# MoBA queries and keys with the rotary halves of four heads in two tiles, and some late steps of a decoder layer moved

## The chip, the cores and the metric

The kernel runs on one core of a Trainium2 chip. The metric is the device time of one execution in microseconds. The core has a matrix engine (TensorE, PE in the profile, with its weight loads shown as PEld), three engines for elementwise work (VectorE = DVE, ScalarE = ACT, GpSimd = POOL) and queues that start transfers (here those of SyncE = SP and of ACT). Each engine works through its own instructions in order and waits for the others by semaphores.

## What is computed

One layer over 512 tokens of width 1024, in float32. Two kinds of attention run side by side from the same normalised input, MoBA with rotary positions and stick-breaking without, with 8 heads of 64 each; they are gated, merged, and followed by a convolutional gated feed-forward of width 2816.

```python
h   = RMSNorm(x)
[q_a,k_a,v_a | q_b,k_b,v_b | gate_a,gate_b] = h @ W_in
y_a = MoBA(rope(q_a), rope(k_a), v_a)
y_b = stick_breaking(q_b, k_b, v_b)
m   = sigmoid(gate_a) * (y_a @ W_a) + sigmoid(gate_b) * (y_b @ W_b)
x   = x + m @ W_out
x   = x + ConvGLU(RMSNorm(x))
out = RMSNorm_final(x)

def rope(t, pos):                      # for each head, 64 wide
    t1, t2 = t[..., :32], t[..., 32:]
    return concat([t1*cos - t2*sin, t2*cos + t1*sin], axis=-1)
```

With 512 tokens and blocks of 256, MoBA's selection takes every past block, so it is causal softmax attention.

## The kernel before

**Number format.** Each float32 operand is split into a rounded part and a residue (`hi`, `lo`, in the format float32r), and each product is three matmuls, hi·hi, hi·lo and lo·hi (`mm3`, L71 to L74). Weights come from HBM in pieces of 128x1024 through `wload` (L55): a transfer to `raw`, a copy to `whi` on ScalarE (L67), the residue `wlo` on VectorE (L68). Three buffers each let the load run ahead of its use.

**Order.** TensorE runs in the order in which the program is written (`manual_schedule`). The order on the other engines is made by a scheduler that simulates the kernel; `tc.issue_after` ties instructions behind a given one on its engine.

**Stages.** (1) Loop over 8 tiles of the input (L161): each tile is scaled and split into `xg`, and 12 matmuls per tile (L184) build MoBA's q and k of the first two head pairs in four PSUM banks `qk0`. Squares of the input are summed in `ssq` (L159), from which `rstd_cols` (8 small matmuls, L117, then a square root and a Newton step) and `bcast_rows` (4 transposes, L136) make the norm `r1` and its broadcast `rb`. `NWARM` small matmuls (L150) run ahead of all this. (2) `vproj_a` projects MoBA's values. (3) Four calls of `attend` (L358), each for two pairs of heads: two of MoBA ("a"), two of stick-breaking ("b").

**One call of attend** goes through three units of query tiles. `score` makes the scores in PSUM tiles `sc`, then the weights with VectorE and ScalarE; `turn` transposes the weights of one pair on TensorE (L375) into a PSUM tile `tp`, of which there is one, and copies it out as `aT` on ScalarE (L378) or VectorE (L380). At the end come the products with the values (L393). After each step, `fill(gap)` issues other projections on TensorE: a filler unit is three 128x512 matmuls. The gaps stand in `GAPS_A`, `GAPS_A2` and `GAPS_B`, the fillers in a list (L424): MoBA's q and k of the other pairs, stick-breaking's q, k and values, and the first `NG` gates.

**MoBA's rotation** (`moba_half`, L256) works on one pair, its two heads one below the other in 128 partitions, the two halves of each head 32 partitions apart. The projection is copied from PSUM to `pc` (L258), four transfers on ScalarE's queue write it with the halves exchanged into `sw` (L261), and VectorE multiplies `pc` by cos (L263) and `sw` by signed sin (L264), adds them (L265) and `split_out` splits the sum (L249, L250). The scores of a head are then matmuls over 64 partitions, the two heads of a pair one after the other (L307).

**Afterwards**: the merge of the two branches (L454 on, with the remaining gates), the output projection, the second norm (`norm2`, L490, after the first up-projection), 44 up-projections with their convolution, and the down-projection. When the attention's PSUM pools close, new ones open: `pmm2` (6 banks) and `ptr2` (2 banks).

Of the kernel before, what the change touches and what calls it, by code (L numbers as in the profile page):

```python
# [10 lines left out]
F32 = mybir.dt.float32  # L11
# [12 lines left out]
FT = FF // 128  # L24
EPS = 1e-6
NG = 3
NWARM = 32
LAST = 4
WORDER = ([(n, k) for n in ("qk0", "va") for k in range(4)] + [("vb", g, h) for g in range(2) for h in range(2)]
          + [("mqk", p, n) for p in (2, 3) for n in range(2)] + [("sqk", p, n) for p in range(4) for n in range(2)]  # L30
          + [("g", i, b) for i in range(KT) for b in range(2)] + [("ab", i) for i in range(KT)]
          + [("out", i) for i in range(KT)] + [("up", i, b) for i in range(FT) for b in range(2)]
          + [("down", k) for k in range(FT)])
# [5 lines left out]
def trunk_layer(ctx: ExitStack, tc: tile.TileContext, xT: bass.AP, w: bass.AP, vec: bass.AP,  # L39
# [3 lines left out]
    def pool(stack, name, bufs, space=None, side=None):  # L43
        kw = {}
        if space is not None:
            kw["space"] = space
        if side is not None:
            kw["side"] = side
        return stack.enter_context(tc.tile_pool(name=name, bufs=bufs, reuse_waits="tile", **kw))
# [5 lines left out]
    def wload(key, pieces=1, dst=None, eng=None):  # L55
        raw = wraw.tile([128, 1024], F32, name="raw")
        hi = (dst or wsp).tile([128, 1024], F32R, name="whi")
        lo = (dst or wsp).tile([128, 1024], F32R, name="wlo")
        n = 1024 // pieces
        for i in range(pieces):  # L60
            sl = slice(i * n, (i + 1) * n)
            (eng if eng is not None and i == 0 else nc.sync).dma_start(raw[:, sl], w[WIDX[key]][:, sl])
            if eng is not None and i == 0:
                nc.scalar.preload_act_table_set("sqrt_and_others")
        for i in range(pieces):
            sl = slice(i * n, (i + 1) * n)
            nc.scalar.activation(hi[:, sl], raw[:, sl], AF.Copy)  # L67
            nc.vector.tensor_sub(lo[:, sl], raw[:, sl], hi[:, sl].bitcast(F32))  # L68
        return hi, lo
# [71 lines left out]

    st1 = ExitStack()
    xp = pool(st1, "xp", 6)
    swp0 = pool(st1, "swp0", 4)
    p1 = pool(st1, "p1", 1, PSUM)
    ssq = xp.tile([128, S], F32, name="ssq", bufs=1)
    qk0 = [p1.tile([128, S], F32, name=f"q{j}") for j in range(4)]
# [13 lines left out]
    for k in range(KT):  # L161
        xk = xks[k] = xp.tile([128, S + 1], F32, name="xk")
        nc.sync.dma_start(xk, xT[k])
        if k % 2 == 0:
            w0 = wload(("qk0", k // 2), 4 if k == 0 else 2, eng=nc.scalar if k == 0 else None)
        if k == 1:
            nc.sync.dma_start(vecs, vec)
        gm = xk[:, S:]
        if k == 0:
            nc.vector.tensor_scalar(xg[k][:, 0], xk[:, :S], gm, None, op0=OP.mult)  # L170
        else:
            xgi = nc.scalar.activation(xg[k][:, 0], xk[:, :S], AF.Copy, scale=gm)
        nc.vector.scalar_tensor_tensor(xg[k][:, 1], xk[:, :S], gm, xg[k][:, 0].bitcast(F32),
                                       op0=OP.mult, op1=OP.subtract)
        if k >= 3:
            with tc.issue_after(xgi.ins):
                square(k - 3)
        if k == KT - 1:
            for j in range(k - 2, KT):
                square(j)  # L180
            r1 = rstd_cols(ssq, pmm, "mm", "n1")
        for n, (i, j) in enumerate(((0, 0), (0, 1), (1, 0))):
            for c in range(4):
                nc.tensor.matmul(qk0[c], w0[i][:, (k % 2) * 512 + c * 128:(k % 2) * 512 + (c + 1) * 128],  # L184
                                 xg[k][:, j], start=(k == 0 and n == 0), stop=(k == KT - 1 and n == 2))
# [19 lines left out]
    mp = pool(mst, "mp", 1, side="right")  # L205
    va = mp.tile([128, QT, 512], F32, name="va")
    rt = pool(mst, "rt", 2, side="right")
    swp = pool(mst, "swp", 2, side="right")
    tg = mp.tile([128, 2, S], F32, name="tg")
    nc.sync.dma_start(tg, trig)  # L210
    for i in range(2):
# [36 lines left out]
    def split_out(hl, o):  # L248
        nc.scalar.activation(hl[:, 0], o, AF.Copy)  # L249
        nc.vector.tensor_sub(hl[:, 1], o, hl[:, 0].bitcast(F32))  # L250

    stk = {}

    mq = {}

    def moba_half(p, n, P, tmp):  # L256
        pc = tmp.tile([128, S], F32, name="pc")
        nc.scalar.activation(pc, P, AF.Copy, scale=(0.125, 1.0)[n])  # L258
        sw = tmp.tile([128, S], F32, name="sw")
        for r in range(0, 128, 32):  # L260
            nc.scalar.dma_start(sw[r:r + 32], pc[r ^ 32:(r ^ 32) + 32])  # L261
        m1 = rt.tile([128, S], F32, name="m1")
        nc.vector.tensor_mul(m1, pc, tg[:, 0])  # L263
        nc.vector.tensor_mul(sw, sw, tg[:, 1])  # L264
        nc.vector.tensor_add(m1, m1, sw)  # L265
        hl = mqkp.tile([128, 2, S], F32R, name=f"hl{n}")
        split_out(hl, m1)
        mq.setdefault(p, []).append(hl)
        if n:
            stk["a", p] = [(*mq[p], h * 64) for h in range(2)]  # L270

    def moba_qk(p):
        for n in range(2):
            yield from proj(("mqk", p, n), lambda ps: moba_half(p, n, ps, swp))

    def sb_qk(p):
        sc = {}
# [16 lines left out]
    def scores(br, pairs, seg):  # L294
        scs = [psc.tile([128, 2, 512], F32, name="sc") for _ in pairs]
        if br == "a":
            for sc in scs:
                for j, (qt, o, n) in enumerate(seg):
                    for h in range(2):
                        nc.tensor.matmul(sc[:, h, o + n - 128:o + n], identb, maskb, start=j == 0, stop=False,  # L300
                                         skip_group_check=True)
        for p, sc in zip(pairs, scs):
            for qt, o, n in seg:
                for m, (c, d) in enumerate(((0, 0), (0, 1), (1, 0))):
                    for h in range(2):
                        q, k, r0 = stk[br, p][h]
                        nc.tensor.matmul(sc[:, h, o:o + n], q[r0:r0 + 64, c, qt * 128:(qt + 1) * 128],  # L307
                                         k[r0:r0 + 64, d, :n], start=br == "b" and m == 0, stop=m == 2,
                                         skip_group_check=True)
        return scs  # L310

    def weights_a(sc, seg):
# [86 lines left out]
            nc.scalar.activation(y[:, 0], av[:, j], AF.Copy)  # L399
            nc.vector.tensor_sub(y[:, 1], av[:, j], y[:, 0].bitcast(F32))  # L400

    for p in range(2):
        for n in range(2):
            moba_half(p, n, qk0[2 * n + p], swp0)
    vproj_a()
    st1.close()
    atp = pool(asta, "atp", 2)
# [13 lines left out]
            yield from proj(("g", i, b), lambda ps: use(b, ps))  # L421

    pend = {}
    fillers = [moba_qk(2), moba_qk(3), sb_qk(0), sb_qk(1), vproj_b(0), sb_qk(2), sb_qk(3), vproj_b(1)]  # L424
    fillers += [gates(i) for i in range(NG)]
    GAPS_A = (14, 0, 4, 6, 0, 4, 8, 4, 4)
    GAPS_A2 = (10, 0, 3, 6, 0, 3, 6, 3, 3)
    GAPS_B = (8, 4, 4, 4, 4, 4, 8, 4, 4)
    attend("a", (0, 1), GAPS_A)
    attend("a", (2, 3), GAPS_A2)  # L430
    mst.close()
# [6 lines left out]
    fill(1000)  # L438
    psA.close()
    psB = ExitStack()  # L440
    pmm = pool(psB, "pmm2", 6, PSUM)
    ptr = pool(psB, "ptr2", 2, PSUM)
    asta.close()

    x1p = pool(ctx, "x1p", 1)
# [41 lines left out]
            nc.vector.tensor_add(ssq2, ssq2, sq)  # L487
    rb2 = x1s.tile([128, S], F32, name="rb2")

    def norm2():  # L490
        r2 = rstd_cols(ssq2, ptr, "tp", "n2")
        bcast_rows(r2, ptr, "tp", rb2)

    upq = [(i, b) for i in range(FT) for b in range(2)]

    def up_mm():
# [4 lines left out]
        return ps  # L501

    ups = [up_mm()]
    norm2()
    ups.append(up_mm())
    mst.close()
    gp = pool(ctx, "gp", 1)
    gT = [gp.tile([128, 2, S], F32R, name=f"gT{i}") for i in range(FT)]
# [73 lines left out]
def pack(w_in, w_a, w_b, w_out, w_up, w_down):  # L582
    def rows(m, c):
        return m[:, c].reshape(m.shape[0] // 128, 128, len(c)).transpose(1, 0, 2).reshape(128, -1)

    c128 = np.arange(128)
    t = {}
    first = np.concatenate([np.arange(256), 512 + np.arange(256)])
    for k in range(4):
        t["qk0", k] = rows(w_in[k * 256:(k + 1) * 256], first)  # L590
    for p in (2, 3):
        for n, base in enumerate((0, 512)):
            t["mqk", p, n] = rows(w_in, base + p * 128 + c128)
    for j in range(4):
        t["va", j] = rows(w_in[j * 256:(j + 1) * 256], 1024 + np.arange(512))
    for g in range(2):
        for h in range(2):
            t["vb", g, h] = rows(w_in[h * 512:(h + 1) * 512], 2560 + g * 256 + np.arange(256))
    for p in range(4):
        for n, base in enumerate((1536, 2048)):  # L600
            t["sqk", p, n] = rows(w_in, base + p * 128 + c128)
    for i in range(KT):
        for b in range(2):
            t["g", i, b] = rows(w_in, 3072 + b * 1024 + i * 128 + c128)
        t["ab", i] = np.concatenate([rows(w_a, i * 128 + c128), rows(w_b, i * 128 + c128)], axis=1)
        t["out", i] = rows(w_out, i * 128 + c128)
    for i in range(FT):
        for b in range(2):
            t["up", i, b] = rows(w_up, b * FF + i * 128 + c128)
        t["down", i] = w_down[i * 128:(i + 1) * 128]  # L610
    return np.ascontiguousarray(np.stack([t[k] for k in WORDER]))
# [29 lines left out]
```

## Time and profile before

| | us |
|---|---|
| median of 3 runs | 758.01 |
| lowest and highest of them | 757.87 and 759.09 |
| profiled execution | 759.67 |
| its span, first to last instruction | 757.6 |

The mean granted TensorE clock of the profiled execution is 0.995 of full. The profile lists, among other things, busy times, groups of instructions by line and form, waits between engines, busy times in chosen stretches (windows) and the timeline of one engine. A line such as `L264 DVE TENSOR_TENSOR sw<-sw,tg 128x512 ... x8 | 5.5, 691 | 8.3 <-DMA sw<-pc 8.3` reads: line 264, on VectorE, tile `sw` from `sw` and `tg`, 8 times; 5.5 us in all, 691 ns each on average; before them the engine was idle for 8.3 us, and what ended that was the transfer of `pc` to `sw`. All stretches are in microseconds from the start of the span.

### The profile page before, as it was taken

The numbers are of one execution on the slowest core, as the hardware profiler recorded it, in microseconds if no ns is written. First come the engines' busy times: TensorE is split into PE (matmuls) and PEld (weight loads), VectorE is DVE, ScalarE is ACT, GpSimd is POOL, SyncE is SP. The second block draws the span as 40 slices with busy tenths as digits, with TensorE's granted clock in tenths as the row PEclk, the third lists the DMA queues.
The fourth block names the chain that finished last, engine by engine and source line by source line (L and its number), as shares of the span: only waits on it lengthen the run. The fifth ranks groups of instructions, "written<-read, shape, count | busy, mean of one in ns | idle before, by whom it ended". The sixth has DMA issues, their size and how long they took to land.

```text
span 757.6 us, 9539 instructions
## 1 busy us (share of the span) xinstructions
PE 738.8 (98%) x3816; PEld 614.7 (81%) x3816; DVE 450.4 (59%) x638; ACT 310.0 (41%) x445; POOL 22.6 (3%) x40
## 2 busy tenths in 40 slices
PE   8999899999999999999989999999999999999996
PEld 7887788969887888888878888888888888888885
DVE  6676767494873544446557767677767773222233
ACT  6445445454662332324345444444444442121233
POOL 0000000220410000000000000000000000000000
PEclk9999999999999999999999999999999999999998
DMA  9433312021125223232322222323232323323203
GB/s 313 137 112 98 90 37 83 30 84 56 57 84 188 91 84 111 84 111 84 112 84 83 96 99 87 109 86 109 86 109 84 112 83 112 105 90 94 101 28 112
DMA packets 23900, 74.12 MB, mean 98 GB/s; under 512 B 2992, under 2 KB 3632, under 8 KB 23856
## 3 DMA queue, kind: packets, MB, share of 16 engines
q1 hardware_dynamic: 21600, 70.24, 27.7%
q10 hardware_dynamic: 2256, 3.28, 1.5%
q8 instruction: 30, 0.49, 0.3%
q14 instruction: 14, 0.11, 0.0%
HBM read 69.31 MB, written 2.10 MB: 94 GB/s over the span
## 4 chain that ended last, share of the span: by engine, by line
PE 73%; issue 20%; DVE 2%; ACT 2%; DMA 1%; POOL 1%; ACTq 0%; POOLq 0%; DVEq 0%
PE mm L72 18%; PE mm L73 18%; PE mm L74 18%; PE d L74 5%; PE d L72 5%; PE d L73 5%; PE q L184 3%; POOL a L338 1%; DMA sw<-pc 1%; DVE R L346 1%; PE tp L393 1%; ACT whi L67 1%; DMA raw<-w 0%; PE d L544 0%; PE tp L375 0%
## 5 line engine op out<-in xcount | busy, mean ns | idle before, releaser
L67 ACT ACTIVATE whi<-raw 128x1024 fp32r<-128x1024 f32 (+2 forms) x128 | 129.8, 1020 | 220.8 <-PE mm L73 78.9
L68 DVE TENSOR_TENSOR wlo<-raw,whi 128x1024 fp32r<-128x1024 f32 (+2 forms) x128 | 150.0, 1176 | 94.3 <-ACT whi L67 93.2
L72 PE MATMUL mm<-h,whi 128*128 128x512 f32 x352 | 137.0, 389 | 0.0
L74 PE MATMUL mm<-h,wlo 128*128 128x512 f32 x352 | 137.0, 389 | 0.0
L73 PE MATMUL mm<-h,whi 128*128 128x512 f32 x352 | 136.9, 389 | 0.0
L72 PE MATMUL mm<-xg,whi 128*128 128x512 f32 x224 | 90.4, 403 | 0.0
L73 PE MATMUL mm<-xg,whi 128*128 128x512 f32 x224 | 87.9, 392 | 0.0
L74 PE MATMUL mm<-xg,wlo 128*128 128x512 f32 x224 | 87.8, 392 | 0.0
L74 PEld LDWEIGHTS mm<-h,wlo 128*128 128x128 f32 x352 | 66.1, 188 | 13.8
L73 PEld LDWEIGHTS mm<-h,whi 128*128 128x128 f32 x352 | 66.1, 188 | 13.7
L72 PEld LDWEIGHTS mm<-h,whi 128*128 128x128 f32 x352 | 66.1, 188 | 13.5
L72 PE MATMUL d<-whi,gT 128*128 128x512 f32 x176 | 69.2, 393 | 0.0
L74 PE MATMUL d<-whi,gT 128*128 128x512 f32 x176 | 68.5, 389 | 0.0
L73 PE MATMUL d<-wlo,gT 128*128 128x512 f32 x176 | 68.5, 389 | 0.0
L517 DVE TENSOR_TENSOR u<-mm,rb 128x512 f32<-128x512 f32 x44 | 30.3, 689 | 41.2 <-PE mm L74 41.2
L72 PEld LDWEIGHTS mm<-xg,whi 128*128 128x128 f32 x224 | 42.5, 190 | 10.0 <-issue 1.4
L74 PEld LDWEIGHTS mm<-xg,wlo 128*128 128x128 f32 x224 | 42.3, 189 | 9.1
L73 PEld LDWEIGHTS mm<-xg,whi 128*128 128x128 f32 x224 | 42.4, 189 | 7.9
L249 ACT ACTIVATE gT<-t 128x512 fp32r<-128x512 f32 x22 | 13.9, 632 | 60.6 <-DVE t L526 60.6
L74 PEld LDWEIGHTS d<-whi,gT 128*128 128x128 f32 x176 | 33.0, 188 | 6.9
L73 PEld LDWEIGHTS d<-wlo,gT 128*128 128x128 f32 x176 | 33.1, 188 | 6.6
L72 PEld LDWEIGHTS d<-whi,gT 128*128 128x128 f32 x176 | 33.1, 188 | 6.4
(180 smaller groups left out, 1046.0 us busy)
## 6 DMA issues: line engine op xcount, KB each, us to landing
raw<-w SPq DMA_DIRECT2D x118, 512.0 KB, 3.3
xk<-xT SPq DMA_DIRECT2D x8, 256.5 KB, 5.4
sw<-pc ACTq DMA_DIRECT2D x32, 64.0 KB, 2.0
x1T<-xT SPq DMA_DIRECT2D x8, 256.0 KB, 5.0
raw<-w SPq DMA_DIRECT2D x6, 256.0 KB, 5.6
out<-on ACTq DMA_DIRECT2D x4, 256.0 KB, 2.7
out<-on SPq DMA_DIRECT2D x4, 256.0 KB, 2.5
tg<-trig SPq DMA_DIRECT2D x1, 512.0 KB, 6.2
```

The lines of the kernel that those rows point to most:

```text
L67: nc.scalar.activation(hi[:, sl], raw[:, sl], AF.Copy)
L68: nc.vector.tensor_sub(lo[:, sl], raw[:, sl], hi[:, sl].bitcast(F32))
L72: nc.tensor.matmul(ps, a[0], b[0], start=start, stop=False)
L73: nc.tensor.matmul(ps, a[0], b[1], start=False, stop=False)
L74: nc.tensor.matmul(ps, a[1], b[0], start=False, stop=stop)
L184: nc.tensor.matmul(qk0[c], w0[i][:, (k % 2) * 512 + c * 128:(k % 2) * 512 + (c + 1) * 128], xg[k][:, j], start=(k == 0 and n == 0), stop=( ...
L249: nc.scalar.activation(hl[:, 0], o, AF.Copy)
L338: nc.gpsimd.affine_select(out=zz, in_=zz, pattern=[[0, 2], [-1, 128]], compare_op=OP.is_ge, fill=fill, base=-1, channel_multiplier=1)
L346: nc.vector.tensor_tensor_scan(R[:, h, r0:r0 + n][:, ::-1], z[:, ::-1], z, 1.0, op0=OP.mult, op1=OP.bypass)
L393: nc.tensor.matmul(av[h * 64:(h + 1) * 64, j, qt * 128:(qt + 1) * 128], v[:, kb, (2 * p + h) * 64:(2 * p + h + 1) * 64], aT[p][:, h, o + k ...
L517: nc.vector.tensor_mul(u, ps, rb2)
```

## The change

- The weights of MoBA's q and k are packed so that one projection holds the first halves of four heads (32 partitions each) and another the second halves. `rotate` multiplies each by cos and by sin straight from PSUM, and when both are there, forms the difference and the sum and splits them. Copy, exchange transfers and `swp` pools are gone.
- MoBA's scores (in `scores`) are matmuls over 32 partitions, four heads in turn, three products for each of the two halves, into four PSUM banks.
- The first weight load is issued after the first tile's split; `NWARM` goes from 32 to 36; `rstd_cols` of the first norm moves behind four matmuls of the last tile; the transposes of the second norm move behind the second up-projection; `ptr2` is opened ahead of `pmm2`; some gaps differ.

```diff
-NWARM = 32
+NWARM = 36
...
     for k in range(KT):
...
-        if k % 2 == 0:
-            w0 = wload(("qk0", k // 2), 4 if k == 0 else 2, eng=nc.scalar if k == 0 else None)
...
         if k == 0:
             nc.vector.tensor_scalar(xg[k][:, 0], xk[:, :S], gm, None, op0=OP.mult)
         else:
+            if k % 2 == 0:
+                w0 = wload(("qk0", k // 2), 2)
             xgi = nc.scalar.activation(xg[k][:, 0], xk[:, :S], AF.Copy, scale=gm)
-        nc.vector.scalar_tensor_tensor(...)
+        xlo = nc.vector.scalar_tensor_tensor(...)
+        if k == 0:
+            with tc.issue_after(xlo.ins):
+                w0 = wload(("qk0", 0), 4, eng=nc.scalar)
...
-            r1 = rstd_cols(ssq, pmm, "mm", "n1")
         for n, (i, j) in enumerate(((0, 0), (0, 1), (1, 0))):
+            if k == KT - 1 and n == 1:
+                r1 = rstd_cols(ssq, pmm, "mm", "n1")
...
-    def moba_half(p, n, P, tmp):
-        pc = tmp.tile([128, S], F32, name="pc")
-        nc.scalar.activation(pc, P, AF.Copy, scale=(0.125, 1.0)[n])
-        sw = tmp.tile([128, S], F32, name="sw")
-        for r in range(0, 128, 32):
-            nc.scalar.dma_start(sw[r:r + 32], pc[r ^ 32:(r ^ 32) + 32])
-        m1 = rt.tile([128, S], F32, name="m1")
-        nc.vector.tensor_mul(m1, pc, tg[:, 0])
-        nc.vector.tensor_mul(sw, sw, tg[:, 1])
-        nc.vector.tensor_add(m1, m1, sw)
-        hl = mqkp.tile([128, 2, S], F32R, name=f"hl{n}")
-        split_out(hl, m1)
...
+    def rotate(g, n, i, ps, half):
+        sc = (0.125, 1.0)[n]
+        half[i] = [rt.tile([128, S], F32, name=f"r{i}{j}") for j in range(2)]
+        for j in range(2):
+            nc.vector.scalar_tensor_tensor(half[i][j], ps, sc, tg[:, j], op0=OP.mult, op1=OP.mult)
+        if i:
+            out = []
+            for j, op in ((0, nc.vector.tensor_sub), (1, nc.vector.tensor_add)):
+                o = half[0][j]
+                op(o, o, half[1][1 - j])
+                hl = mqkp.tile([128, 2, S], F32R, name=f"hl{j}")
+                split_out(hl, o)
+                out.append(hl)
+            stk.setdefault(("a", g), []).append(out)
+
+    def moba_qk(g):
+        for n in range(2):
+            half = {}
+            for i in range(2):
+                yield from proj(("mqk", n, i), lambda ps: rotate(g, n, i, ps, half))
...
+            Q, K = stk["a", pairs[0] // 2]
+            for qt, o, n in seg:
+                for i in range(2):
+                    for m, (c, d) in enumerate(((0, 0), (0, 1), (1, 0))):
+                        for h in range(4):
+                            r0 = h * 32
+                            nc.tensor.matmul(scs[h // 2][:, h % 2, o:o + n],
+                                             Q[i][r0:r0 + 32, c, qt * 128:(qt + 1) * 128], K[i][r0:r0 + 32, d, :n],
+                                             start=False, stop=i == 1 and m == 2, skip_group_check=True,
+                                             tile_position=(r0, 0))
+            return scs
...
-    fillers = [moba_qk(2), moba_qk(3), sb_qk(0), sb_qk(1), vproj_b(0), sb_qk(2), sb_qk(3), vproj_b(1)]
+    fillers = [moba_qk(1), sb_qk(0), sb_qk(1), vproj_b(0), sb_qk(2), sb_qk(3), vproj_b(1)]
...
-    GAPS_A = (14, 0, 4, 6, 0, 4, 8, 4, 4)
+    GAPS_A = (12, 0, 5, 5, 0, 5, 7, 5, 5)
     GAPS_A2 = (10, 0, 3, 6, 0, 3, 6, 3, 3)
-    GAPS_B = (8, 4, 4, 4, 4, 4, 8, 4, 4)
+    GAPS_B = (8, 4, 5, 4, 3, 5, 7, 5, 5)
...
+    ptr = pool(psB, "ptr2", 2, PSUM)
     pmm = pool(psB, "pmm2", 6, PSUM)
-    ptr = pool(psB, "ptr2", 2, PSUM)
...
     ups = [up_mm()]
-    norm2()
+    r2 = rstd_cols(ssq2, ptr, "tp", "n2")
     ups.append(up_mm())
+    bcast_rows(r2, ptr, "tp", rb2)
...
-    first = np.concatenate([np.arange(256), 512 + np.arange(256)])
+    def halves(base, g, i):
+        return base + (4 * g + c128 // 32) * 64 + 32 * i + c128 % 32
+
+    first = np.concatenate([halves(base, 0, i) for base in (0, 512) for i in range(2)])
```

More of the change, by code (lines that the diff above doesn't have):

```diff
@@ L26 @@
 NG = 3
-NWARM = 32
+NWARM = 36
 LAST = 4
 WORDER = ([(n, k) for n in ("qk0", "va") for k in range(4)] + [("vb", g, h) for g in range(2) for h in range(2)]
-          + [("mqk", p, n) for p in (2, 3) for n in range(2)] + [("sqk", p, n) for p in range(4) for n in range(2)]
+          + [("mqk", n, i) for n in range(2) for i in range(2)] + [("sqk", p, n) for p in range(4) for n in range(2)]
           + [("g", i, b) for i in range(KT) for b in range(2)] + [("ab", i) for i in range(KT)]
@@ L143, in trunk_layer @@
     xp = pool(st1, "xp", 6)
-    swp0 = pool(st1, "swp0", 4)
     p1 = pool(st1, "p1", 1, PSUM)
@@ L171, in trunk_layer @@
         else:
+            if k % 2 == 0:
+                w0 = wload(("qk0", k // 2), 2)
             xgi = nc.scalar.activation(xg[k][:, 0], xk[:, :S], AF.Copy, scale=gm)
-        nc.vector.scalar_tensor_tensor(xg[k][:, 1], xk[:, :S], gm, xg[k][:, 0].bitcast(F32),
-                                       op0=OP.mult, op1=OP.subtract)
+        xlo = nc.vector.scalar_tensor_tensor(xg[k][:, 1], xk[:, :S], gm, xg[k][:, 0].bitcast(F32),
+                                             op0=OP.mult, op1=OP.subtract)
+        if k == 0:
+            with tc.issue_after(xlo.ins):
+                w0 = wload(("qk0", 0), 4, eng=nc.scalar)
         if k >= 3:
@@ L207, in trunk_layer @@
     rt = pool(mst, "rt", 2, side="right")
-    swp = pool(mst, "swp", 2, side="right")
     tg = mp.tile([128, 2, S], F32, name="tg")
@@ L252, in trunk_layer @@
     stk = {}
-    mq = {}
-    def moba_half(p, n, P, tmp):
-        pc = tmp.tile([128, S], F32, name="pc")
-        nc.scalar.activation(pc, P, AF.Copy, scale=(0.125, 1.0)[n])
-        sw = tmp.tile([128, S], F32, name="sw")
-        for r in range(0, 128, 32):
-            nc.scalar.dma_start(sw[r:r + 32], pc[r ^ 32:(r ^ 32) + 32])
-        m1 = rt.tile([128, S], F32, name="m1")
-        nc.vector.tensor_mul(m1, pc, tg[:, 0])
-        nc.vector.tensor_mul(sw, sw, tg[:, 1])
-        nc.vector.tensor_add(m1, m1, sw)
-        hl = mqkp.tile([128, 2, S], F32R, name=f"hl{n}")
-        split_out(hl, m1)
[L268 to L272, printed above, removed]
+    def rotate(g, n, i, ps, half):
[13 more added lines that the diff above has]
+    def moba_qk(g):
         for n in range(2):
-            yield from proj(("mqk", p, n), lambda ps: moba_half(p, n, ps, swp))
+            half = {}
+            for i in range(2):
+                yield from proj(("mqk", n, i), lambda ps: rotate(g, n, i, ps, half))
     def sb_qk(p):
@@ L307, in scores @@
                         nc.tensor.matmul(sc[:, h, o:o + n], q[r0:r0 + 64, c, qt * 128:(qt + 1) * 128],
-                                         k[r0:r0 + 64, d, :n], start=br == "b" and m == 0, stop=m == 2,
-                                         skip_group_check=True)
+                                         k[r0:r0 + 64, d, :n], start=m == 0, stop=m == 2, skip_group_check=True)
         return scs
@@ L400, in attend @@
             nc.vector.tensor_sub(y[:, 1], av[:, j], y[:, 0].bitcast(F32))
-    for p in range(2):
-        for n in range(2):
-            moba_half(p, n, qk0[2 * n + p], swp0)
+    for n in range(2):
+        half = {}
+        for i in range(2):
+            rotate(0, n, i, qk0[2 * n + i], half)
     vproj_a()
@@ L488, in trunk_layer @@
     rb2 = x1s.tile([128, S], F32, name="rb2")
-    def norm2():
-        r2 = rstd_cols(ssq2, ptr, "tp", "n2")
-        bcast_rows(r2, ptr, "tp", rb2)
     upq = [(i, b) for i in range(FT) for b in range(2)]
@@ L587, in pack @@
     t = {}
-    first = np.concatenate([np.arange(256), 512 + np.arange(256)])
+    def halves(base, g, i):
+        return base + (4 * g + c128 // 32) * 64 + 32 * i + c128 % 32
+    first = np.concatenate([halves(base, 0, i) for base in (0, 512) for i in range(2)])
     for k in range(4):
         t["qk0", k] = rows(w_in[k * 256:(k + 1) * 256], first)
-    for p in (2, 3):
-        for n, base in enumerate((0, 512)):
-            t["mqk", p, n] = rows(w_in, base + p * 128 + c128)
+    for n, base in enumerate((0, 512)):
+        for i in range(2):
+            t["mqk", n, i] = rows(w_in, halves(base, 1, i))
     for j in range(4):
@@ L629 @@
     ang = np.tile(inv, 4)[:, None] * np.arange(S, dtype=np.float32)[None, :]
-    sign = np.where(np.arange(128) % 64 < 32, -1, 1).astype(np.float32)[:, None]
-    trig = np.ascontiguousarray(np.stack([np.cos(ang), sign * np.sin(ang)], axis=1).astype(np.float32))
+    trig = np.ascontiguousarray(np.stack([np.cos(ang), np.sin(ang)], axis=1).astype(np.float32))
     arrays = {"xT": xT, "w": w, "vec": vec, "gfin": np.ascontiguousarray(a["g_final"]), "trig": trig}
```

## The prediction

> **What bounds the kernel now.** I read the page's busy times first.
>
> ```profile
> PE 738.8 (98%) x3816; PEld 614.7 (81%) x3816; DVE 450.4 (59%) x638; ACT 310.0 (41%) x445; POOL 22.6 (3%) x40
> ```
>
> TensorE (PE) is busy for 98% of the span. Matmuls follow one another without a pause nearly everywhere, so an engine other than PE matters only where it makes PE wait. The price of a plain matmul and one of those waits stand in the chain of work that ended last (start, duration, what).
>
> ```profile
> 387.97 0.23 PE mm L73
> 388.20 0.23 PE mm L74
> ...
> 390.67 1.28 ACT L124
> 391.96 0.21 ACT n2s L124
> ...
> 393.03 0.65 PE tp L136 x4
> ```
>
> One 128x512 matmul advances the chain by 0.23 us, so a projection of 24 takes 5.5 us and one unit of filler (three matmuls) 0.68 us. The second view is the waits of PE alone (total, times, longest).
>
> ```profile
> PE tp L375 <- ACT aT L378: 3.9, 3, 2.0
> PE tp L136 <- DVE n2r L130: 2.5, 1, 2.5
> PE tp L375 <- DVE aT L380: 1.9, 1, 1.9
> PE q L184 <- ACT whi L67: 1.1, 1, 1.1
> PE mm L72 <- DVE g L416: 0.8, 1, 0.8
> PE tp L393 <- DVE aT L380: 0.6, 1, 0.6
> ```
>
> That is nearly all: 10.8 us. The third view is the windows table around these places (stretch, its length, then busy time and count of PE, PEld, DVE, ACT, POOL, the granted clock, DMA share, GB/s).
>
> ```profile
> 4.64:5.77 1.13, 0.01 (x1) 0.03 (x1) 0.93 (x3) 1.05 (x4) 0.00 (x0) 1.00 1.01 303
> 5.77:9.35 3.58, 3.58 (x9) 2.84 (x10) 2.96 (x6) 1.76 (x3) 0.00 (x0) 1.00 0.94 262
> 69.50:72.00 2.50, 0.63 (x4) 0.21 (x3) 2.50 (x5) 1.04 (x2) 0.00 (x0) 1.00 0.00 0
> 81.50:84.30 2.80, 0.76 (x4) 0.30 (x4) 2.40 (x4) 2.15 (x5) 0.00 (x0) 1.00 0.49 184
> 84.30:88.00 3.70, 3.70 (x13) 3.15 (x14) 2.96 (x8) 2.50 (x6) 0.00 (x0) 0.54 0.00 0
> 158.00:161.00 3.00, 1.28 (x9) 0.82 (x9) 3.00 (x4) 2.03 (x3) 0.48 (x1) 1.00 0.00 0
> ```
>
> PE is idle for 1.13 us before its first real matmul, 1.87 us before 72 and 2.04 us before 84.3 (first attention call), and 1.72 us near 160 (third call). The fifth row holds a cost that no wait shows: PE is busy throughout, but at a granted clock of 0.54, which loses about 3.7 x 0.46 = 1.7 us. The second row hides the same: nine matmuls in 3.58 us are 0.40 us each instead of 0.23, 1.5 us lost, though the clock column has no lower record there. So 14 us of the span is PE that could run and doesn't, and the rest is work.
>
> **The change, part by part.** *Rotation without transfers.* What PE waited for at 72 is seen in VectorE's timeline (start, duration, line, form, idle time before and its releaser).
>
> ```profile
> 65.89 0.96 DVE L316 TENSOR_REDUCE st<-sc 128x2 f32<-128x768 f32 x1 [1.26 <-PE sc L307]
> 68.71 0.69 DVE L264 TENSOR_TENSOR sw<-sw,tg 128x512 f32<-128x512 f32 x1 [1.86 <-DMA sw<-pc]
> ...
> 70.18 0.68 DVE L265 TENSOR_TENSOR m<-m,sw 128x512 f32<-128x512 f32 x1
> 70.78 0.95 DVE L380 COPY aT<-tp 128x768 f32<-128x768 f32 x1
> ```
>
> The copy at 70.78 is what PE waits for; in front of it on the in-order engine stands a multiplication that waited 1.86 us for the exchanged halves. The same happens before 84.3, one engine further on (first VectorE, then ScalarE):
>
> ```profile
> 77.62 0.69 DVE L264 TENSOR_TENSOR sw<-sw,tg 128x512 f32<-128x512 f32 x1 [1.11 <-DMA sw<-pc]
> ...
> 82.01 0.69 ACT L320 ACTIVATE a<-sc,st 128x512 f32<-128x512 f32 x1 [2.30 <-DVE st L316]
> ...
> 83.35 0.81 ACT L378 ACTIVATE aT<-tp 128x768 f32<-128x768 f32 x1
> ```
>
> The prices of the removed and added operations are in the groups by form (busy, mean ns, idle) and in the tile view of `sw` (ns: min/median/max).
>
> ```profile
> L261 ACTq DMA_DIRECT2D sw<-pc x32: 514/602/613, 31.6 to 92.7; - x32
> L264 DVE TENSOR_TENSOR sw<-sw,tg 128x512 f32<-128x512 f32 x8 | 5.5, 691 | 8.3 <-DMA sw<-pc 8.3
> L258 ACT ACTIVATE pc<-mm 128x512 f32<-128x512 f32 x4 | 2.4, 593 | 0.0
> L282 DVE SCALAR_TENSOR_TENSOR o<-mm,rb 128x512 f32<-128x512 f32 x4 | 2.7, 676 | 0.0
> L250 DVE TENSOR_TENSOR hl<-m,hl 128x512 fp32r<-128x512 f32 x8 | 5.4, 686 | 0.1
> ```
>
> Removed: eight copies on ScalarE (8 x 0.59 = 4.8 us), 32 DMA issues from its queue (32 x 0.60 = 19 us of sequencer time) and 8.3 us in which VectorE stood still. VectorE's own work stays: per half three elementwise operations and a split residue before (4 x 0.69), and per two halves four products read from PSUM (4 x 0.68), two sums and two residues now. New: a product reads PSUM itself, so a projection's bank is held until VectorE gets there; the bank is wanted two projections on, 5.5 us after the next one starts, and the ordinary use at L282 already works like that. Behind the products stand weight residues and reductions, which wait for no transfer any more. The idle time in this call is 1.87 + 2.04 + 0.6 us, with the 1.7 us at low clock 6.2 us. Not all goes: both pairs' scores now end together, so the first reduction starts up to 0.8 us later, and VectorE's load stays dense (2.50 of 2.50 and 2.40 of 2.80 us in the windows above). The bounds are 0 and -6.2; I take **-4.2**, near the full end because the waits named are removed outright and the gaps there grow from 4 units to 5.
>
> *Scores from 32-row slices.* The time of today's 64-row matmuls is in the windows table for their line (PE, PEld).
>
> ```profile
> 53.50:55.10 1.60, 1.60 (x24) 1.42 (x24) 1.00 0.05 20
> 65.05:66.31 1.26, 1.26 (x12) 1.00 (x12) 1.00 0.97 263
> 76.95:78.53 1.58, 1.58 (x12) 1.04 (x12) 1.00 0.00 0
> ...
> sum 8.85, PE 8.84 PEld 6.93; mean PE 1.47 PEld 1.15
> ```
>
> In the third row twelve 512-column matmuls take 1.58 us: 0.13 each, half of a plain one. So two heads on different row halves run at once, and a pair-step (two heads, one product) costs what one matmul costs. The new loop has twice the matmuls, in groups of four heads with 32 rows each, over two halves: 2 x 3 = 6 groups where 2 pairs x 3 = 6 pair-steps stood. If four run at once the time is the same; if two at a time, +8.85 us; if one at a time, four times as long, +26.5 us. If it is the issue that limits (first row: 48 instructions in 1.60 us, 33 ns each), 96 in the first unit take 3.2 and 48 in the second 1.6, hence 2 x (1.6 + 0.34) = +3.9 us. No row shows four, but a group is the same form as the pair, split further; I take **+0.5**, bounds 0 and +26.5. [...]
>
> *Start.* Before, VectorE's order was (start, duration, operation):
>
> ```profile
> 4.80 0.42 DVE L68 TENSOR_TENSOR wlo<-raw,whi 128x256 fp32r<-128x256 f32 x1 [2.83 <-ACT whi L67]
> 5.15 0.48 DVE L170 TENSOR_SCALAR xg<-xk 128x512 fp32r<-128x512 f32 x1
> ```
>
> The first matmul (5.77) comes after the product at 5.15, which stands behind a residue that is needed eight matmuls later. With the order reversed the product starts between 4.35 and 4.80: 0.35 to 0.8 us, I take -0.6. The weight load keeps its place on both DMA queues (nothing was issued between it and the input tile). Four more warm-up matmuls close what is left of the 1.13 us gap, and the slow stretch after it may shorten: 0 to -1.5, I take -1.2. [...] The norm's column sums move behind four matmuls, which hides a wait of 0.2 us; the chain from square root to the last VectorE step took 1.0 us in the second norm, and eight matmuls (1.8 us) still cover it. Together **-2.0**, bounds 0 and -2.6.
>
> *Second norm.* What follows it runs like this stretch of the up-projection:
>
> ```profile
> 500.00:600.00 100.00, 100.00 (x443) 82.84 (x442) 72.96 (x93) 44.87 (x55) 0.00 (x0) 1.00 0.30 100
> ```
>
> Its transposes move behind the second up-projection: the 2.5 us wait goes, and 5.5 us of matmuls cover the chain, table load included. Late next: the first evacuations, some 3 us, with six PSUM banks (32 us of matmuls) and VectorE at 73% busy there. No DMA moves. **-2.5**, bounds -2.5 and -1.
>
> *Exchanged PSUM pools.* The first merge matmul no longer takes the bank that the last gate (L416) still reads: **-0.8**, bounds 0 and -0.8. The ten filler units after the last attention call become six; the transfers in SP's queue keep their order there.
>
> *Gaps of the stick-breaking calls.* On ScalarE, the copy that PE awaits near 160 stood behind these:
>
> ```profile
> 158.29 0.63 ACT L249 ACTIVATE hl<-o 128x512 fp32r<-128x512 f32 x1 [3.25 <-DVE o L282]
> 158.83 0.79 ACT L334 ACTIVATE a<-sc 128x768 f32<-128x768 f32 x1
> ```
>
> One unit more in that gap covers 0.68 us of 1.72; the order itself is the scheduler's. **-0.8**, bounds +1 (a stall elsewhere, where a gap shrinks by one unit) and -1.72.
>
> Sum: -4.2 + 0.5 - 2.0 - 2.5 - 0.8 - 0.8 = -9.8 us. The profiled execution took 759.67 us (span 757.6), which gives 749.9; the median of the runs is 758.01, which gives 748.2. I predict **748.5**, nearer to the median.
>
> **The rivals.** *Issue-bound groups*: the matmuls of a group follow each other at the 33 ns of the first score row; for it speaks that no row shows a shorter mean, against it that the 512-column rows show the overlap whole. +3.4 on the forecast: 751.9. *The stalls come back*: VectorE stays dense in the first call and the scheduler puts other work ahead of the copies, so the terms -4.2 and -0.8 fail: 753.5. Against it: 8.3 us of standing still are gone. *Two at a time*: 748.5 + 8.35 = 756.9. *One at a time, the slower side*: the array takes 32-row slices in turn, in the score loop of the two MoBA calls, +26.0: 774.5. It outweighs the 10.3 us gained elsewhere once a group takes over 2.2 pair-steps. Against it: the 64-row pairs overlap completely. *The change doesn't do what it says* would be exchange waits replaced by waits of the sums for the second half; both halves come from one engine in order, so it only joins the second rival.
>
> **How the numbers follow.** Forecast 62% (own range 744 to 752), issue-bound 15%, stalls back 8%, two at a time 8%, one at a time 7%. A measurement here can tell 0.2% (1.5 us) from no change, so faster means below 756.5: 62 + 15 + 8 = 85%; within: 8%; slower: 7%. The range 743.5 to 755.5 holds the first three and leaves out 15% and a little of the tails; its lower end is a sum with most terms at their full size.
>
> **What would show it.** Right: no VectorE wait on a DMA in the first 105 us; PE waits at L375 below 3 us in all; no stretch at clock 0.54 near 85; PE's wait at L136 gone; the score line's windows near 8.9 us in all. Wrong: score windows of 12 us or more (groups don't overlap), new waits at L375 or for PSUM banks behind the products, or a first matmul still near 5.8.

## The result, and the profile after

The changed kernel takes 746.56 us (median of 4 runs, 746.23 to 746.70), the kernel before 758.55 us beside it (757.87 to 759.32). The ratio is 0.9841 with an interval of 0.9824 to 0.9858: 12 us, or 1.6%, faster. The profiled execution took 746.50 us, its span 744.8 us against 757.6.

The page's first part, and the waits of PE (total, times, longest), of the changed kernel:

```profile
PE 735.4 (99%) x3916; PEld 613.2 (82%) x3916; DVE 448.8 (60%) x638; ACT 305.9 (41%) x437; POOL 21.6 (3%) x40
```

```profile
PE tp L386 <- ACT aT L389: 1.7, 2, 1.0
PE mm L149 <- DVE warmb L87: 1.1, 1, 1.1
```

Of the waits shown before, only 1.7 us at the transposes are left, in the second and the third attention call (the 1.1 us are the wait for the first instruction of all, and stood there before too). PE's busy time hardly fell; what went is idle time and time at a low clock. Cut into stretches by the starts of the same matmuls, the two profiled executions differ so:

| stretch (us) | before | after | after, units evened out | difference |
|---|---|---|---|---|
| start to first score | 53.48 | 51.27 | 51.27 | -2.2 |
| first call, score to value product | 46.53 | 39.93 | 39.93 | -6.6 |
| to the value product of the second call | 38.98 | 39.58 | 39.58 | +0.6 |
| to that of the fourth call | 91.19 | 92.92 | 90.20 | -1.0 |
| to the output projection | 110.48 | 106.65 | 109.37 | -1.1 |
| output projection | 43.52 | 43.52 | 43.52 | 0.0 |
| up-projections | 243.29 | 240.78 | 240.78 | -2.5 |

(Four filler units, 4 x 0.68 = 2.72 us, moved from behind the fourth call into the third and fourth; the fourth column takes that out.) Half of the gain lies in the first call.

The scores from 32-row slices cost what the 64-row ones did. The windows table for their line (stretch, length, PE, PEld), first call and sum of both:

```profile
51.27:52.88 1.61, 1.61 (x48) 1.45 (x48) 1.00 0.00 0
61.48:62.73 1.25, 1.25 (x24) 1.00 (x24) 1.00 0.00 0
71.29:72.89 1.60, 1.60 (x24) 1.10 (x24) 1.00 0.46 184
...
sum 8.89, PE 8.88 PEld 7.09; mean PE 1.48 PEld 1.18
```

Twice the instructions stand in the same 1.60 us: 24 matmuls of 512 columns take 0.067 us each on average, where a plain one takes 0.23, and start in groups of four, each group within 0.03 us, so four run at once; the sum is 8.89 us against 8.85. The 48 matmuls of the first row take 1.61 us, not the 3.2 us of groups bound by their issue.

VectorE in the place where it had waited for the exchanged halves (start, duration, line, form, idle time before):

```profile
62.94 1.82 DVE L327 TENSOR_REDUCE st<-sc 128x2 f32<-128x768 f32 x2
64.67 0.95 DVE L391 COPY aT<-tp 128x768 f32<-128x768 f32 x1
```

The reductions and the copy that PE needs follow each other without idle time; the copy ends at 65.6 and PE wants it at 66.89, after its fifth filler unit. The start, again on VectorE and then on PE:

```profile
4.21 0.49 DVE L167 TENSOR_SCALAR xg<-xk 128x512 fp32r<-128x512 f32 x1 [2.24 <-DMA xk<-xT]
4.74 0.75 DVE L172 SCALAR_TENSOR_TENSOR xg<-xk,xg 128x512 fp32r<-128x512 f32 x1
5.40 1.43 DVE L68 TENSOR_TENSOR wlo<-raw,whi 128x256 fp32r<-128x256 f32 x4
```

```profile
1.05 4.02 PE L149 MATMUL mm<-warmb 128*128 128x128 bf16 x36 [1.05 <-DVE warmb L87]
4.88 2.70 PE L187 MATMUL q<-xg,whi 128*128 128x512 f32 x8
```

The first product starts when the input lands, and PE goes from the warm-up to real matmuls without a gap; the first eight take 2.7 us instead of 3.7.

### The profile page after: what moved, and what is told of

Same layout as the page of the kernel before. It is cut to its first block, busy times and chain, and to the rows that moved or that the text cites. A ratio compares the mean times of both kernels' runs of the same rounds, so it can differ in the third digit from the quotient of the medians.

```text
span 744.8 us, 9682 instructions
## 1 busy us (share of the span) xinstructions
PE 735.4 (99%) x3916; PEld 613.2 (82%) x3916; DVE 448.8 (60%) x638; ACT 305.9 (41%) x437; POOL 21.6 (3%) x40
## 4 chain that ended last, share of the span: by engine, by line
PE 79%; issue 19%; DVE 1%; ACT 0%; POOL 0%; POOLq 0%; DVEq 0%; ACTq 0%
PE mm L72 20%; PE mm L73 20%; PE mm L74 20%; PE d L74 5%; PE d L73 5%; PE d L72 5%; PE tp L404 1%; PE tp L386 1%; PE sc L319 1%; DVE R L357 1%; PE d L553 0%; DVE a L359 0%; DVE wlo L68 0%; PE tp L117 0%; DVE on L587 0%
```

## The experiments

All runs below are the changed kernel with one edit, except where said. Some were made on other chips, where the kernel before took 760.5 us in the median, so each has its ratio to the kernel before measured beside it.

**The changed kernel again.**

> The changed kernel again, unaltered, as the base of the others on the same chip. Every theory: within 1 us of 746.6.

746.42 us, ratio 0.9821 (0.9795 to 0.9847). It is the base for the differences below.

**Rotation and scores only.** Everything else of the change is put back:

```diff
-NWARM = 36
+NWARM = 32
-    GAPS_A = (12, 0, 5, 5, 0, 5, 7, 5, 5)
+    GAPS_A = (14, 0, 4, 6, 0, 4, 8, 4, 4)
-    GAPS_B = (8, 4, 5, 4, 3, 5, 7, 5, 5)
+    GAPS_B = (8, 4, 4, 4, 4, 4, 8, 4, 4)
...
-    ups.append(up_mm())
     bcast_rows(r2, ptr, "tp", rb2)
+    ups.append(up_mm())
```

(and the first weight load, the first norm's sums and the PSUM pools as before).

> The changed kernel with every late step, the start, the PSUM pools and the gaps put back, so that only the rotation and the 32-row scores are left of the change. My theory, from the two traces: the first attention call keeps its 6.6 us, and what comes back is 2.2 us at the start, 2.5 us at the second norm, 1.1 us at the merge and about 1 us in the calls with other gaps, hence 753 to 754 us. Rival (the larger gaps, not the missing exchange, emptied the first call): PE waits at the transposes again by 3 us or more and the time is 756 us or more.

757.0 us, ratio 0.9951 (0.9933 to 0.9969): slower than I expected, and both signs of the rival are there, waits of 4.2 us at the transposes and a time above 756 us. Waits of PE, and one window behind the second norm (PE, PEld, DVE, ACT, POOL, clock):

```profile
PE tp L383 <- ACT aT L386: 4.2, 3, 1.8
PE tp L136 <- DVE n2r L130: 2.5, 1, 2.5
```

```profile
389.40:393.00 3.60, 3.55 (x12) 3.05 (x13) 1.48 (x3) 0.81 (x1) 0.00 (x0) 0.59 0.36 138
```

The wait at 72 is gone, but one of 1.8 us is left where there was one of 2.0, and the 2.5 us wait at the norm is followed by a stretch at clock 0.59, which loses another 1.5 us (3.6 x 0.41). The first call takes 41.95 us here, with full clock: without the low-clock loss of 1.7 us that the profile before has there (46.53), the rotation alone is worth 2.9 us in it, and 2.0 us are missing to the 39.93 of the whole change. So the gaps have a part of their own. What stands in front of the wait that is left, on VectorE, ScalarE and PE in turn:

```profile
76.46 1.28 DVE L257 SCALAR_TENSOR_TENSOR r<-mm,tg 128x512 f32<-128x512 f32 x2
77.65 1.21 DVE L68 TENSOR_TENSOR wlo<-raw,whi 128x1024 fp32r<-128x1024 f32 x1
78.79 2.34 DVE L324 TENSOR_REDUCE st<-sc 128x2 f32<-128x1024 f32 x2
...
80.11 0.69 ACT L328 ACTIVATE a<-sc,st 128x512 f32<-128x512 f32 x1 [4.12 <-DVE st L324]
...
81.45 0.81 ACT L386 ACTIVATE aT<-tp 128x768 f32<-128x768 f32 x1
...
82.32 0.87 PE L383 MATMUL tp<-ident,a 128*128 128x128 f32 x6 [1.84 <-ACT aT L386]
```

No transfer is left here and VectorE isn't idle: the new products and a weight residue stand ahead of the reductions. In the changed kernel, with five units in the gap, the reductions start at 73.00, right behind the scores, and PE doesn't wait.

**Old gaps in the changed kernel, and new gaps in the kernel before.**

```diff
-    GAPS_A = (12, 0, 5, 5, 0, 5, 7, 5, 5)
+    GAPS_A = (14, 0, 4, 6, 0, 4, 8, 4, 4)
-    GAPS_B = (8, 4, 5, 4, 3, 5, 7, 5, 5)
+    GAPS_B = (8, 4, 4, 4, 4, 4, 8, 4, 4)
```

> The old gaps in the changed kernel, all else as changed. My theory (rotation and gaps share the first call's 6.6 us; the run with the rotation only had one wait of 2.0 us left there): about 2 us more in the first call and 1 us in the calls after it, 749 to 750.5 us. Rival (the gaps are worth nothing once the transfers are gone): below 747.5 us.

751.52 us, ratio 0.9880 (0.9866 to 0.9895), 5 us above the changed kernel and 1 us above my range, which left out the clock. A wait of 2 us is back in the first call, and with it the low clock (window, then PE's waits):

```profile
80.00:84.00 4.00, 3.91 (x13) 3.37 (x14) 1.25 (x5) 2.19 (x6) 0.00 (x0) 0.57 0.01 4
```

```profile
PE tp L386 <- ACT aT L389: 4.3, 3, 2.0
```

```diff
-    GAPS_A = (14, 0, 4, 6, 0, 4, 8, 4, 4)
+    GAPS_A = (12, 0, 5, 5, 0, 5, 7, 5, 5)
-    GAPS_B = (8, 4, 4, 4, 4, 4, 8, 4, 4)
+    GAPS_B = (8, 4, 5, 4, 3, 5, 7, 5, 5)
```

> The kernel before with the new gaps and nothing else. My theory (the wait for the exchanged halves is longer than one unit of filler can cover): PE waits of 2 us or more at the transposes of the first call remain, about 1 to 2.5 us gained in all, 756 to 758 us. Rival (one unit more in each gap is enough by itself): the first call's waits go and the time is below 753 us.

754.15 us, ratio 0.9916 (0.9901 to 0.9930). My range is missed, on the rival's side: the new gaps alone do more for the time than the rotation alone. (Part of that lies elsewhere: 1.0 us in the stick-breaking calls, whose gaps are new too, and the 1.5 us of low clock at the norm, which only the rotation's profile has.) The tile view of `sw` (what ended the idle time in front of it) and the waits of PE:

```profile
  DMA sw<-pc: 5.7, 5
```

```profile
PE tp L375 <- ACT aT L378: 2.1, 3, 1.0
...
PE tp L375 <- DVE aT L380: 0.4, 1, 0.4
```

VectorE still stands still for 5.7 us behind the transfers, yet PE's waits at the transposes fall from 5.8 us to 2.5 us over all calls, and the clock reads 1.00 from 80 to 84 us, where the run before this one has 0.57. The first call takes 41.64 us. One unit of filler (0.68 us) more in the gaps and a shorter first gap cover most of a 1.9 us delay (which of the two does how much was not tested apart), and the loss of clock behind the wait of 2 us doesn't occur.

**Exchange transfers without a reader, and with one.** 32 transfers on ScalarE's queue are put back, four for each tile that the sums take from the second half. In the first run nothing reads them; in the second VectorE's sums do. (For room, the products of the second half have one buffer in both.)

```diff
+                sw = swp.tile([128, S], F32, name="sw")
+                for r in range(0, 128, 32):
+                    nc.scalar.dma_start(sw[r:r + 32], half[1][1 - j][r:r + 32])
-                op(o, o, half[1][1 - j])
+                op(o, o, sw)            # second run only
```

> The changed kernel with 32 transfers of 64 KB put back on ScalarE's queue, four for each second-half product, into a tile that nothing reads. My theory (VectorE's wait for the exchanged halves was the cost, not their issue): PE's waits in the first call stay below 1 us and the time is 746 to 748 us. Rival (19 us of issue time in ScalarE's in-order queue delay its copies): 749 to 752 us.

> The same transfers, but the sums on VectorE read the transferred tiles, so that VectorE waits for them as it did before the change. My theory: 4 us or more of VectorE waits on these transfers, PE waits at the transposes of the first call again, 749 to 752 us. Rival (issue alone matters): the same time as with the unread transfers, within 0.5 us.

Unread: 748.42 us, ratio 0.9846 (0.9824 to 0.9867). Read: 761.24 us, ratio 1.0013 (0.9999 to 1.0028). Idle time in the tile view of the second run and PE's waits there:

```profile
  DMA sw<-r: 12.5, 5
```

```profile
PE tp L390 <- ACT aT L393: 6.4, 3, 4.8
PE sc L313 <- ACT hl L252: 3.1, 2, 2.4
PE sc L313 <- DVE hl L253: 1.4, 2, 1.1
```

The unread transfers cost 2 us, more than I expected, and PE waits for 1.6 us in the first call where I expected less than 1 us; the rival's figure was nearer. The first call is 41.69 us long: the splits on ScalarE stand behind the issues. (VectorE also waits for 1.1 us, once, for the single buffer; that is at 43 us, where PE doesn't wait.) The wait costs 13 us more, above both expectations: here the transfers start after VectorE's products instead of after ScalarE's copy, so they come later than in the kernel before, even the first scores wait for them, and the run says more about a chain of VectorE, queue, transfer and VectorE than about the old kernel's price.

**Order of the heads.** All six products of a head at a stretch, and two heads in turn before the other two:

```diff
-                for i in range(2):
-                    for m, (c, d) in enumerate(((0, 0), (0, 1), (1, 0))):
-                        for h in range(4):
+                for h in range(4):
+                    for i in range(2):
+                        for m, (c, d) in enumerate(((0, 0), (0, 1), (1, 0))):
```

> MoBA's scores in another order: all six products of one head, then the next head, so that neighbouring matmuls use the same 32 rows. My theory (four slices run at once only because the heads take turns): the 24 matmuls of 512 columns take 24 x 0.227 = 5.4 us instead of 1.6, those of the other units 4 to 5.5 instead of 1.25 and 1.61, in both calls together 21 to 23 us more, hence 766 to 770 us. Rival (a 32-row matmul is short whatever runs beside it): no change, 746 to 748 us.

```diff
-                for i in range(2):
-                    for m, (c, d) in enumerate(((0, 0), (0, 1), (1, 0))):
-                        for h in range(4):
+                for hp, i, (m, (c, d)) in [(hp, i, mm) for hp in range(2) for i in range(2)
+                                           for mm in enumerate(((0, 0), (0, 1), (1, 0)))]:
+                        for h in (2 * hp, 2 * hp + 1):
```

> MoBA's scores with two heads in turn, then the other two. My theory: only two slices overlap, the score windows double from 8.9 us to 17.8 us, hence about 755 us. Rival (four overlap however they are ordered, since the weights of the next matmuls are loaded ahead): 746 to 748 us.

756.58 us (754.48 to 758.73), ratio 0.9949 (0.9933 to 0.9965), and 748.82 us, ratio 0.9853 (0.9831 to 0.9875). Both cost far less than expected. The third unit's 24 matmuls of 512 columns, first heads one after another, then two at a time:

```profile
73.59:76.89 3.30, 3.30 (x24) 2.75 (x24) 1.00 0.22 86
```

```profile
72.18:74.35 2.17, 2.17 (x24) 1.64 (x24) 1.00 0.38 153
```

In turn they took 1.60 us. So the order matters and taking turns is the best of the three, but with six matmuls in a row on the same 32 rows each took 0.14 us (3.30 / 24), well below the 0.23 of one at a time. The median of the first run (10 us above the base) is more than its scores explain: the profiled execution, at 754.48 us, is the fastest of its runs, and its first two calls are 4.6 and 4.0 us longer than the base's. The others have no trace, but their clock is on record: the runs above 756 us had a mean granted clock of 0.994 to 0.996, those below had 0.998 or 0.999.

**Second norm back.**

```diff
-    ups.append(up_mm())
     bcast_rows(r2, ptr, "tp", rb2)
+    ups.append(up_mm())
```

> The second norm's transposes back ahead of the second up-projection, all else as changed. My theory: PE's wait of 2.5 us returns, 749 us, or 750 us if the granted clock drops behind the idle time as it did with the rotation only. Rival (the chain is hidden by the banks anyway): 746.5 us.

750.78 us (749.27 to 750.97), ratio 0.9872 (0.9849 to 0.9896). Windows across and behind the wait:

```profile
378.00:382.80 4.80, 2.35 (x16) 2.02 (x14) 1.97 (x6) 2.54 (x3) 0.00 (x0) 1.00 0.24 77
382.80:387.00 4.20, 4.20 (x14) 3.39 (x15) 2.58 (x4) 0.81 (x1) 0.00 (x0) 0.59 0.30 115
```

2.45 us of waiting, and 4.20 x 0.41 = 1.7 us at low clock, which the profile before didn't have behind the same wait. The step is worth 2.5 us, or 4.1 where the clock falls; the fastest run, 1.5 us below the others, is about what the first case gives.

**Start back, and 32 warm-up matmuls only.** The first run puts the first weight load ahead of the first tile's split again and takes the four extra warm-up matmuls away; the second takes away only those.

```diff
+        if k == 0:
+            w0 = wload(("qk0", 0), 4, eng=nc.scalar)
...
-            with tc.issue_after(xlo.ins):
-                w0 = wload(("qk0", 0), 4, eng=nc.scalar)
...
-NWARM = 36
+NWARM = 32
```

> The first weight load back ahead of the first tile's split and 32 warm-up matmuls, all else as changed. My theory: the first matmul is 0.9 to 1.1 us later and the slow first stretch returns in full (about 1.3 us), 748.5 to 749 us. Rival (the later stages wait for the input transfers, which arrive at the same time): below 747.3 us.

> 32 warm-up matmuls instead of 36, all else as changed. My theory (the order of the first product, not the warm-up, moves the first matmul; the four extra ones only close the gap ahead of it): the first matmul still near 4.9, a gap of 0.4 us ahead of it, and in most executions a slow stretch of up to 3.4 us more, so 746.5 to 748.2 us with a wider spread between runs than 0.5 us. Rival (the first matmul's time alone counts): 746.5 us with the usual spread.

748.51 us (746.60 to 748.80), ratio 0.9842 (0.9817 to 0.9866), and 746.50 us (746.25 to 746.89), ratio 0.9814 (0.9798 to 0.9830). The order is worth 2 us in three runs of four; the four warm-up matmuls can't be told from nothing, and the wider spread that I expected of them isn't there. The profiled execution of the first run is its fastest, 746.60 us, and shows why one run escapes:

```profile
5.76:9.35 3.59, 3.59 (x16) 2.96 (x17) 3.17 (x7) 2.20 (x4) 0.00 (x0) 1.00 0.96 288
```

The first matmul is as late as before (5.76), but 16 of them run in the stretch that held 9 in the kernel before: 0.22 us each, against 0.40 there. The first clock record of the kernel before is full clock from 9.35 us, that of the changed kernel full clock from 6.15 us. (The clock column reads 1.00 ahead of the first record too, so the low clock shows only in the matmuls' 0.40 us.) The first scores start at 51.36 us in this execution, and in the changed kernel's second profile at 51.36 us too: the 0.9 us by which the first matmul comes earlier buy nothing there. That the order buys its 2 us by the clock is read from these three traces; the three slower runs have none.

**The waits that are left.** One filler unit goes ahead of the second call's fourth transposes, and in the third call alone two go ahead of the second pair's first ones:

```diff
-    GAPS_A2 = (10, 0, 3, 6, 0, 3, 6, 3, 3)
+    GAPS_A2 = (10, 0, 3, 6, 0, 4, 5, 3, 3)
     GAPS_B = (8, 4, 5, 4, 3, 5, 7, 5, 5)
+    GAPS_B1 = (6, 4, 7, 4, 3, 5, 7, 5, 5)
...
-    attend("b", (0, 1), GAPS_B)
+    attend("b", (0, 1), GAPS_B1)
```

> The changed kernel with two of the remaining waits aimed at: one filler unit moved ahead of the second call's fourth transposes, and in the third call two units moved ahead of the second pair's first transposes. My theory: the waits of 0.7 and 1.0 us at the transposes shrink to 0.3 us in all, 745 to 745.6 us. Rival (the scheduler's other order or a later transposition takes it back): 746.2 us or more.

744.38 us (743.88 to 744.47), ratio 0.9786 (0.9771 to 0.9801): faster than both kernels, 2.0 us below the change, and 0.6 us below the range that I expected. All waits of PE in its profile:

```profile
PE mm L149 <- DVE warmb L87: 1.1, 1, 1.1
PE mm L117 <- DVE ssq L158: 0.4, 1, 0.4
```

No wait at a transpose is left. The new gaps also changed the scheduler's order on ScalarE: the copy in the third call now stands ahead of the split that had held it up.

## Why the prediction was right or wrong

The time was right: 748.5 was predicted in 743.5 to 755.5, 746.56 was measured, and none of the rivals (751.9 us and more) occurred. The terms add up to -9.8 us, the two profiled executions differ by 12.8.

- *Scores* (+0.5): +0.04, four slices at once. The prices of the alternatives, +8.85 and +26.5 us, were not put to the test, since four slices do run at once when the heads take turns (0.067 us each). The two other orders were expected to bring these cases about, as if matmuls on different rows overlapped only when they are neighbours; that was wrong, and the third unit took 2.17 and 3.30 us, not 3.2 and 5.4.
- *First call* (-4.2, full end -6.2): -6.6, the term that was mis-sized: 2.4 of the 3.0 us that the sum lacks. The reason given, "the waits named are removed outright and the gaps there grow from 4 units to 5", put the exchange first and the gaps last. The reading "The same happens before 84.3" did not hold: without any transfer, and with the old gaps, that wait is still 1.84 us long, behind VectorE work without idle time, and the larger gap takes it away. The runs share the term out so: the rotation alone takes 2.9 us from the first call, the new gaps alone 3.2 (46.53 - 1.7 - 41.64), both together 4.9, since they overlap, and 1.7 us is the low clock (0.54) behind the wait of 2.04 us. That VectorE's wait for transfers causes PE's wait is shown for the one at 72, which goes with the rotation alone; but as much of the cure could be had without removing the transfers. That the term came out at its full end and no worse is partly luck: the gaps, the reason named last, took the wait that the rotation left.
- *Start* (-2.0): -2.2. The order of VectorE's first steps does it, but not as the sum has it (0.6 us for the earlier matmul, 1.2 us for the clock with the warm-up's help): the earlier matmul bought nothing in the execution whose first 16 matmuls took 0.22 us each, and the four warm-up matmuls show no effect of their own. With the new order the first record of full clock begins at 6.15 us instead of 9.35.
- *Second norm* (-2.5): -2.5 in the two profiles. Put back, it cost 4 us in most runs, 1.7 of them for the clock.
- *PSUM pools* (-0.8): -1.1 in the two profiles, the wait of 0.8 us and what follows it. No run tests it alone.
- *Stick-breaking gaps* (-0.8): -1.0; with the old gaps in the changed kernel the stretch is 91.19 us again. The wait at 160 shrank by just the one unit, from 1.72 to 1.04 us, since the order on ScalarE stayed the same, as the last experiment confirms by changing it.
- *Not predicted*: the second call is 0.6 us longer. This goes with the rotation and the scores, not with the gaps: 39.57 us with the rotation only, 38.99 with the new gaps alone. Its wait at the fourth transposes grew, probably because both pairs' scores end together and the reduction of the first pair starts later; that is argued from the timeline, not tested.

## What to carry to other kernels

Where one engine is busy all the time, list its waits and ask of each what stands in front of the releasing instruction on its in-order engine; but before the cause is rebuilt, try one filler step more in front of the wait, for it may be the cheaper half of the gain. When a cause is gone, measure again: the next thing on the same engine can hold the wait nearly as long (1.84 us where 2.04 stood). The wait of 2.04 us on TensorE in the kernel before cost 3.7 with the 1.7 us at low clock behind it, so the few long waits come first. Heads or other small products that use different row slices belong in turn in the instruction order: 1.60 us here, against 2.17 and 3.30 in the two other orders.

## What the runs showed of the hardware

- Matmuls on different 32-row slices overlapped fourfold: in the changed kernel's third unit they start in groups of four, and from the second group on the groups follow each other 0.23 us apart, as single full matmuls do (0.067 us each over the whole unit). With six on one slice ahead of the first on another they took 0.14 us each. If only neighbouring heads overlapped there, at most one matmul in six would; by an estimate from these numbers that makes 24 x 0.23 less 3 x 0.23 = 4.8 us, and 3.30 were measured. How the overlap comes about in that order was not shown.
- In the kernel before the granted clock is on record as full from 9.35 us, as half from 84.44, which is 22 times 3.413 us later, and as full again from 87.86, 3.41 us later. The stretches below are of this length; they hold the waits of 1.87, 2.04 and 2.46 us in the kernel before, then the wait of 2.5 us at the second norm with the rotation only and with the new gaps alone (stretch, its length, PE busy, clock, DMA share, GB/s):

```profile
70.79:74.20 3.41, 2.41 (x14) 1.00 0.16 37
81.03:84.44 3.41, 1.37 (x8) 1.00 0.60 183
84.44:87.85 3.41, 3.41 (x12) 0.50 0.00 0
388.23:391.64 3.41, 2.34 (x15) 1.00 0.27 106
391.64:395.06 3.42, 2.03 (x11) 1.00 0.40 153
```

```profile
385.52:388.94 3.42, 1.48 (x12) 1.00 0.03 12
388.94:392.35 3.41, 2.90 (x9) 0.50 0.44 154
```

```profile
385.60:389.02 3.42, 1.55 (x9) 1.00 0.44 152
389.02:392.43 3.41, 3.41 (x17) 1.00 0.02 6
```

Two of these stretches were followed by half clock, those with PE busy for 1.37 and 1.48 us; the one with 1.55 us (new gaps alone) was followed by full clock. The wait of 2.46 us in the kernel before lies in two stretches, with PE busy for 2.34 and 2.03 us, and the clock stayed full; with the rotation only a wait as long was followed by clock 0.50. So this part of the gain differs between executions; what decides it was not shown beyond these rows. The changed kernel's runs lie within 0.5 us, those of the kernel before within 4.7 us (757.72 to 762.44, with a mean clock of 0.995 in the first and 0.991 in the last).
- A 64 KB transfer between parts of the on-chip memory held ScalarE's queue for 0.60 us at its issue (median of 32), and 32 of them that nobody reads cost 2 us (748.42 against 746.42).
